# Splitting keys, values, queries and the output projections' weights once, in the first phase, and keeping both parts in DRAM

## The chip, the cores and the metric

The kernel runs on one core of one Trainium2 chip. The metric is the device time of one execution in microseconds (us), the median of several runs. A core has TensorE (PE, matmuls; PEld is its weight load), VectorE (DVE), ScalarE (ACT), GpSimd (POOL) and SyncE (SP), which here only issues DMAs. Loads are issued on SP's queue, stores mostly on ScalarE's.

## What is computed

One block of two layers over 2048 latent tokens of 1024 channels, with 256 context tokens:

```python
# layer 0 (w_in = attn_in_w, w_out = attn_out_w)
px = modulate(x, g0, shift, scale) @ w_in       # latent; ctx the same, keys and values alone
qA, kA = rms_norm(q), rms_norm(k) per head      # 4 query heads, 2 key heads of 128; rotary positions
oA = softmax(qA kA^T / sqrt(128)) vA            # over latent and context keys
oB = rms_norm((softmax(q1 k1^T / 8) - lam * softmax(q2 k2^T / 8)) vB)   # 4 differential heads
x = x + gate0 * ((concat(oA, oB) * silu(g)) @ w_out)
# layer 1 (w_fout = fourier_out_w)
u, g = split(modulate(x, g1, shift, scale) @ fourier_in_w)
f = real(fft2(u over positions and the 256 channels of each of 4 groups))
x = x + gate1 * ((f * silu(g)) @ w_fout)
out = rms_norm(x, final_g)
```

## The kernel before

Every float32 product is made of three matmuls: both operands are split into a high part (the value rounded to the matmul's format, written by a copy) and a low part (what is left, a subtraction), and `mm3` adds high x high, low x high and high x low (lines 58 to 60). `split` (line 47) makes the parts; its arguments say which engine copies and which subtracts.

The work runs in phases, one after the other on TensorE, with the tile framework's scheduler placing instructions on each engine and each queue in program order by its own estimate, outside the attention phase:

- Phase 1, the input projections, to about 813 us. Two halves of the tokens; within a half the column chunks kva (keys and values of A), kb, vb, qa, qb, and two of the gate. An output tile of 128 tokens x 512 columns takes 24 matmuls into one of five PSUM tiles `mm`. `evac` then normalises, applies the rotary tables and transposes through TensorE (`tr`, `put_T`), and stores to DRAM: keys and queries of A and queries of B in float32 (tile `qT`), keys of B already as high and low stacked (`kTh`, `kTl`), values in float32 (tile `vv`, a ring of three shared with the streamed modulation weights `aw` and the gate tile `sg`). Most of phase 1's extra work on modulation lies here too (`ada_fill`).
- Phase 2, attention, about 814 to 1998 us: 32 steps (4 heads x 8 pairs of 128 queries), whose order on PE, ACT and DVE is written out by hand. SP's queue and GpSimd are not in that order. Keys, values and queries are loaded in float32 and split here, mostly on GpSimd (`load_split`, `load_q`, lines 488 and 508).
- Phase 3, output projection and second modulation, to about 2200 us; phase 4, the Fourier input projection, to 2511 us; phase 5, the transform over positions (`m`, `ae`, `bo` on PE; `g`, `FM` on DVE; `FL` on POOL), to 2558 us; phase 6, the last projection and norm.
- Both output projections load their weights in float32 (`load_wres`, line 736): `w0h`/`w0l` are split for phase 3, and `w1h`/`w1l` for phase 6, there after a multiplication of `wr` by layer 1's gate on GpSimd (line 747). Layer 0's gate is applied after the matmul (`gx`, line 766). Weights come in two halves of columns, c = 0 and c = 1; `out_proj` goes through all four token tiles of c = 0 first.

In phase 6, TensorE takes the projection's row blocks in the order 0, 4, 1, ...; block 4 needs the row `uy`, which needs the four small loads `gy` and then a DMA of that row into `u` (lines 1087 to 1104).

Of the kernel before, what the change touches and what calls it, by code (L numbers as in the profile page):

```python
# [89 lines left out]
def block_kernel(ctx: ExitStack, tc: tile.TileContext, a):  # L90
# [12 lines left out]
    kA_d = dt_("kA", [P, 2, L])  # L103
    kB_d = dt_("kB", [P, 4, 2, L])
    qA_d = dt_("qA", [P, 4, N])
    qB_d = dt_("qB", [P, 4, N])
    vA_d = dt_("vA", [P, 2, LT, P])
    vB_d = dt_("vB", [P, 4, LT, P])
# [138 lines left out]
    with ExitStack() as ph:  # L247
# [9 lines left out]
        vvp = ph.enter_context(tc.tile_pool(name="p1v", bufs=3, reuse_waits="tile"))  # L257
# [71 lines left out]
        def put_T(src, dsts, t, stack=False):  # L329
# [14 lines left out]
            o = wk.tile([P, 4, P], F32, name="qT", tag="qT", bufs=2)  # L344
            S.copy(o[:, 0:nh, :], tr[:, 0:nh, :])
            st(dsts[:, :, t * P:(t + 1) * P], o[:, 0:nh, :])

        def evac(kind, ps, t, rp):

            if kind in ("kva", "qa"):  # L350
# [7 lines left out]
                if kind == "kva":  # L358
                    v = vvp.tile([P, 512], F32, name="vv", tag="vv")
                    S.copy(v[:, 0:256], ps[:, 256:512])  # L360
                    st(vA_d[:, :, t, :], v[:, 0:256].rearrange("p (h d) -> p h d", h=2))
# [8 lines left out]
            else:  # L370
                v = vvp.tile([P, 512], F32, name="vv", tag="vv")
                S.copy(v, ps)
                st(vB_d[:, :, t, :], v.rearrange("p (h d) -> p h d", h=4))
# [15 lines left out]
        def ada_fill(n):  # L389
# [6 lines left out]
            del later[:n]  # L396

        chunks = [("kva", COL_KVA), ("kb", COL_KB), ("vb", COL_VB), ("qa", COL_QA), ("qb", COL_QB),
                  ("g", COL_G), ("g", COL_G + 512)]
        for half in range(2):  # L400
# [5 lines left out]
            for kind, col in chunks:  # L406
                whi, wlo = load_w(col)
                for src, g in groups:
# [17 lines left out]
                    for i in range(4 if src == 0 else 2):  # L426
# [7 lines left out]
                        if kind == "vb" and src == 0:  # L434
                            ada_fill(1)

# [38 lines left out]
    with ExitStack() as ph:  # L475
# [12 lines left out]
        def load_split(pool, src, name, eng=(None, None)):  # L488

            hs, ls = [], []  # L490
            for i in range(3):
                lo = pool.tile([P, KP], F32R, name=name + "l", tag="kv")
                ld(lo.bitcast(F32), src[:, i * KP:(i + 1) * KP])
                hi = pool.tile([P, KP], F32R, name=name + "h", tag="kv")
                split(nc, hi, lo, lo.bitcast(F32), eng[0] or Q, eng[1] or Q)
                hs.append(hi)
                ls.append(lo)
            return hs, ls
# [9 lines left out]
        def load_q(rows, tag, eng=(None, None)):  # L508

            ql = qp.tile([P, QT], F32R, name="ql", tag=tag + "l")  # L510
            n = P // len(rows)
            for r, src in enumerate(rows):
                ld(ql[r * n:(r + 1) * n, :].bitcast(F32), src)
            qh = qp.tile([P, QT], F32R, name="qh", tag=tag + "h")
            split(nc, qh, ql, ql.bitcast(F32), eng[0] or Q, eng[1] or Q)
            return qh, ql
# [140 lines left out]
        def load_keys(h, eng=(None, None)):  # L657
            if h % 2 == 0:
                hd["kA"] = load_split(kp, kA_d[:, h // 2, :], "kA", eng)
            hd["kB"] = [load_stack(kB_d[:, h, c, :], "kB") for c in range(2)]  # L660

        def load_values(h):
            if h % 2 == 0:
                hd["vA"] = load_split(vp, vA_d[:, h // 2].rearrange("p t d -> p (t d)"), "vA")
            hd["vB"] = load_split(vp, vB_d[:, h].rearrange("p t d -> p (t d)"), "vB")

        def load_qs(h, pr, eng=(None, None)):
            qsl = slice(pr * QT, (pr + 1) * QT)
            return (load_q([qA_d[:, h, qsl]], "qa", eng),
                    [load_q([qB_d[c * 64:(c + 1) * 64, h, qsl]] * 2, f"qb{c}", eng) for c in range(2)])  # L670
# [7 lines left out]
        tasks, pairs, items, qs = [], [], [], [load_qs(0, 0, (S, V))]  # L678

        def begin(n):  # L680

            h, pr = steps[n]
            if pr == 0:
                load_keys(h, (S, V) if n == 0 else (None, None))
# [51 lines left out]
    def load_wres(pool, gpool, pools, src, l, order, lo_eng):  # L736
# [4 lines left out]
        for c in range(2):  # L741
            cs = slice(c * 512, (c + 1) * 512)
# [495 lines left out]
```

## Time and profile before

| | |
|---|---|
| Median of 3 runs | 2757.02 us (2750.46, 2757.02, 2762.67) |
| Profiled execution, its own time | 2757.23 us |
| Its span, first to last instruction | 2755.5 us |
| Mean granted TensorE clock | 0.971 of full |
| Busy: TensorE, VectorE, ScalarE, GpSimd | 94%, 66%, 51%, 46% |
| HBM read, written | 220.59 MB, 83.95 MB |

The span is what the rows below are read from; the profiled execution's own time is 1.7 us more. Busy time of an engine is a mean over phases with different limits, so the rows are taken by phase.

### The profile page before, as it was taken

What the parts mean: (1) busy time and instruction counts of PE and PEld (TensorE: products, weight loads), DVE (VectorE), ACT (ScalarE), POOL (GpSimd) and SP (SyncE); (2) the same over time, 40 slices, a digit from 0 to 9 for tenths busy, and PEclk for the clock granted to TensorE, in tenths of its full rate; (3) what the DMA queues carried; (4) which work ended last, traced back from release to release, by engine and by line L of the source; (5) the groups of instructions that cost most, each with busy time, mean ns of one, the idle gap of its engine ahead of it and who ended that gap; (6) DMA issues with size and microseconds to landing.
All of it is one profiled execution on the core that took longest, in us unless ns stands there. A gap on an engine that the chain in (4) does not pass through costs nothing. (4 is left out here: it accounts for less than half of the span.)

```text
span 2755.5 us, 44386 instructions
## 1 busy us (share of the span) xinstructions
PE 2595.3 (94%) x15209; PEld 2257.9 (82%) x15209; DVE 1808.4 (66%) x3855; ACT 1416.1 (51%) x3742; POOL 1259.4 (46%) x1216
## 2 busy tenths in 40 slices
PE   4889999999998999999999999999899899988898
PEld 2778887787877999999989999999778788777687
DVE  6653634747318888888888888888864535464654
ACT  3531222512227888788878888888733522121212
POOL 3121331224218666766887777766432322245200
PEclk7899999999999999999999999999999999999899
DMA  9346345364420001100120001000386767663442
GB/s 302 113 136 171 111 127 190 107 167 134 153 89 20 20 19 55 35 19 20 51 72 20 20 21 60 19 20 15 115 280 216 234 203 225 215 196 118 142 142 92
DMA packets 233457, 307.49 MB, mean 112 GB/s; under 512 B 21552, under 2 KB 134912, under 8 KB 233232
## 3 DMA queue, kind: packets, MB, share of 16 engines
q1 hardware_dynamic: 131536, 224.89, 25.8%
q10 hardware_dynamic: 97472, 75.55, 8.8%
q0 software_dynamic: 4224, 4.21, 0.7%
q8 instruction: 121, 1.98, 0.3%
q14 instruction: 104, 0.85, 0.1%
HBM read 220.59 MB, written 83.95 MB: 111 GB/s over the span
## 5 line engine op out<-in xcount | busy, mean ns | idle before, releaser
L543 DVE TENSOR_REDUCE m<-s 128x1 f32<-128x512 f32 (+1 forms) x960 | 578.5, 632 | 167.4 <-PE s L535 162.9
L555 ACT ACTIVATE e<-s,nm 128x512 f32<-128x512 f32 (+1 forms) x960 | 615.1, 654 | 53.0 <-DVE nm L547 49.7
L639 ACT CAST th<-ptr 128x512 fp32r<-128x512 f32 x576 | 340.8, 592 | 138.1 <-PE ptr L635 123.2
L643 DVE TENSOR_TENSOR tl<-ptr,th 128x512 fp32r<-128x512 f32 x576 | 379.2, 681 | 37.3 <-ACT th L639 37.3
L635 PE MATMUL ptr<-ident,e 128*128 128x128 f32 x2304 | 349.0, 274 | 20.4 <-DVE tl L643 14.2
L597 POOL TENSOR_TENSOR e<-e 128x768 f32<-128x768 f32 x189 | 342.8, 1843 | 0.0
L635 PEld LDWEIGHTS ptr<-ident,e 128*128 128x128 f32 x2304 | 271.5, 141 | 49.2 <-issue 8.4
L535 PE MATMUL s<-kB,qh 128*128 128x512 f32 (+1 forms) x768 | 284.5, 380 | 7.3 <-ACT e L555 7.3
L51 POOL TENSOR_SCALAR whi<-wraw 128x1024 fp32r<-128x1024 f32 (+1 forms) x104 | 122.5, 1181 | 360.8 <-PE mm L59 156.3
L58 PE MATMUL mm<-whi,ghi 128*128 128x512 f32 x688 | 270.8, 397 | 7.7 <-ACT vv L360 5.5
L60 PE MATMUL mm<-whi,glo 128*128 128x512 f32 x688 | 272.2, 397 | 3.8 <-DVE glo L54 3.8
L59 PE MATMUL mm<-wlo,ghi 128*128 128x512 f32 x688 | 270.8, 395 | 0.0
L594 POOL TENSOR_SCALAR e<-e,rs 128x768 f32<-128x768 f32 x192 | 171.0, 913 | 216.8 <-DVE rs L570 216.8
L535 PE MATMUL s<-kB,ql 128*128 128x512 f32 (+1 forms) x768 | 251.4, 340 | 0.0
L312 POOL TENSOR_TENSOR t<-qn,rope 128x256 f32<-128x256 f32 (+1 forms) x128 | 116.7, 934 | 263.1 <-issue 107.7
L54 DVE TENSOR_TENSOR wlo<-wraw,whi 128x1024 fp32r<-128x1024 f32 (+1 forms) x104 | 137.0, 1321 | 150.3 <-POOL whi L51 150.2
L555 ACT ACTIVATION_READ_ACCUMULATOR e<-s,nm 128x1 f32 x960 | 201.9, 210 | 0.0
L594 POOL TENSOR_SCALAR e<-e,c 128x768 f32<-128x768 f32 x189 | 169.1, 912 | 25.9 <-DVE c L578 17.4
L58 PE MATMUL pv<-th,vAh 128*128 128x256 f32 x576 | 170.7, 296 | 0.2 <-ACT oT L608 0.2
L58 PE MATMUL pv<-th,vBh 128*128 128x256 f32 x576 | 165.4, 287 | 0.0
L59 PE MATMUL pv<-tl,vAh 128*128 128x256 f32 x576 | 161.7, 281 | 0.0
L60 PE MATMUL pv<-th,vAl 128*128 128x256 f32 x576 | 161.6, 281 | 0.0
(353 smaller groups left out, 6489.9 us busy)
## 6 DMA issues: line engine op xcount, KB each, us to landing
wraw<-in_w_in SPq DMA_DIRECT2D x56, 512.0 KB
hraw<-h SPq DMA_DIRECT2D x96, 256.0 KB
aw<-in_adaT SPq DMA_DIRECT2D x64, 256.0 KB
g<-sg ACTq DMA_DIRECT2D x64, 256.0 KB
gl<-g SPq DMA_DIRECT2D x64, 256.0 KB
wraw<-in_wg SPq DMA_DIRECT2D x64, 256.0 KB
kB<-kB SPq DMA_DIRECT2D x24, 384.0 KB
awr<-in_adaT SPq DMA_DIRECT2D x32, 256.0 KB
```

The lines of the kernel that those rows point to most:

```text
L54: (lo_eng or nc.vector).tensor_tensor(out=lo, in0=src, in1=hi.bitcast(F32), op=ALU.subtract)
L58: nc.tensor.matmul(out, lh, rh, start=start, stop=False)
L59: nc.tensor.matmul(out, lh, rl, start=False, stop=False)
L60: nc.tensor.matmul(out, ll, rh, start=False, stop=stop)
L535: T.matmul(ps[:, c - o:c - o + cw], l, r[c // KP][:, k:k + cw], start=(j == 0), stop=(j == len(self.terms) - 1))
L543: V.tensor_reduce(out=self.m3[:, i:i + 1], in_=self.segs[i][:, 0:SEG[i][1]], axis=AX.X, op=ALU.max)
L555: S.activation(self.e[:, o:o + w], self.segs[i][:, 0:w], AF.Exp, bias=self.nm, accum_out=self.s3[:, i:i + 1])
L594: eng.tensor_scalar(out=self.e[:, sg], in0=self.e[:, sg], scalar1=by, scalar2=1.0, op0=ALU.mult, op1=ALU.mult)
L597: eng.tensor_tensor(out=onto[:, sg], in0=onto[:, sg], in1=self.e[:, sg], op=ALU.add)
L635: T.transpose(self.tr[:, k, i, :], self.p.es[i][:, kt * P:(kt + 1) * P], ident)
L639: S.copy(self.th, self.tr.rearrange("p k i q -> p k (i q)"))
L643: V.tensor_tensor(out=self.tl, in0=self.tr.rearrange("p k i q -> p k (i q)"), in1=self.th.bitcast(F32), op=ALU.subtract)
```

## The change

Keys and queries of A, queries of B, and all values are split in phase 1, straight from PSUM, and both parts are stored. `w_out` and `w_fout` are loaded, split and stored too: one tile of 128x512 for each of 32 output tiles of phase 1's second half (`wout_fill`, in the chunks kva, kb, qa and qb). Attention and the output projections load both parts and split nothing. Layer 1's gate is now applied after the matmul, as layer 0's is. The ring that holds `vv` grows from three buffers to four and serves six kinds of tile: `vvh`, `vvl`, `wol`, `woh`, `aw`, `sg`.

```diff
-    kA_d = dt_("kA", [P, 2, L])
+    kA_d = pair_("kA", [P, 2, L])          # two DRAM tiles: name + "h", name + "l"
...
-        vvp = ph.enter_context(tc.tile_pool(name="p1v", bufs=3, reuse_waits="tile"))
+        vvp = ph.enter_context(tc.tile_pool(name="p1v", bufs=4, reuse_waits="tile"))
...
-            o = wk.tile([P, 4, P], F32, name="qT", tag="qT", bufs=2)
-            S.copy(o[:, 0:nh, :], tr[:, 0:nh, :])
-            st(dsts[:, :, t * P:(t + 1) * P], o[:, 0:nh, :])
+            hl = [wk.tile([P, 4, P], F32R, name=nm, tag="qT", bufs=2)[:, 0:nh, :] for nm in ("qTh", "qTl")]
+            split(nc, *hl, tr[:, 0:nh, :], S)
+            for o, dst in zip(hl, dsts):
+                st(dst[:, :, t * P:(t + 1) * P], o.bitcast(F32))
+
+        def put_v(src, dsts, t, nh):
+            hl = [vvp.tile([P, 512], F32R, name=nm, tag="vv")[:, 0:nh * P] for nm in ("vvh", "vvl")]
+            split(nc, *hl, src, S)
+            for o, dst in zip(hl, dsts):
+                st(dst[:, :, t, :], o.bitcast(F32).rearrange("p (h d) -> p h d", h=nh))
...
+        def wout_fill(n):
+            for l, i, src in wouts[:n]:
+                lo = vvp.tile([P, 512], F32R, name="wol", tag="vv")
+                ld(lo.bitcast(F32), src)
+                hi = vvp.tile([P, 512], F32R, name="woh", tag="vv")
+                split(nc, hi, lo, lo.bitcast(F32), S)
+                for dst, o in zip(wo_d[l], (hi, lo)):
+                    st(dst[i], o.bitcast(F32))
+            del wouts[:n]
...
                         if kind == "vb" and src == 0:
                             ada_fill(1)
+                        elif half == 1:
+                            wout_fill(1)
...
-        def load_split(pool, src, name, eng=(None, None)):
+        def load_parts(pool, srcs, name):
...
             for i in range(3):
-                lo = pool.tile([P, KP], F32R, name=name + "l", tag="kv")
-                ld(lo.bitcast(F32), src[:, i * KP:(i + 1) * KP])
-                hi = pool.tile([P, KP], F32R, name=name + "h", tag="kv")
-                split(nc, hi, lo, lo.bitcast(F32), eng[0] or Q, eng[1] or Q)
+                for ts, src, p in zip(out, srcs, "hl"):
+                    t = pool.tile([P, KP], F32R, name=name + p, tag="kv")
+                    ld(t.bitcast(F32), src[:, i * KP:(i + 1) * KP])
...
-                raw = pool.tile([P, 512], F32, name="wr", tag="wr", bufs=4)
-                ld(raw, src[kt * P:(kt + 1) * P, cs])
-                if l:
-                    Q.tensor_tensor(out=raw, in0=raw, in1=gate[:, cs], op=ALU.mult)
-                h = pools[c].tile([P, 512], F32R, name=f"w{l}h{kt}{c}", tag=f"h{kt}{c}", bufs=1)
-                lo = pools[c].tile([P, 512], F32R, name=f"w{l}l{kt}{c}", tag=f"l{kt}{c}", bufs=1)
-                split(nc, h, lo, raw, S, lo_eng[c])
+                for src, p in zip(wo_d[l], "hl"):
+                    t = pools[c].tile([P, 512], F32R, name=f"w{l}{p}{kt}{c}", tag=f"{p}{kt}{c}", bufs=1)
+                    ld(t.bitcast(F32), src[c * KT + kt])
...
-                if gate is not None:
-                    t = lp.tile([P, 512], F32, name="gx", tag="gx", bufs=2)
-                    V.tensor_tensor(out=t, in0=ps, in1=gate[:, cs], op=ALU.mult)
-                    ps = t
-                add.tensor_tensor(out=x[i][:, cs], in0=ps, in1=x[i][:, cs], op=ALU.add)
+                t = lp.tile([P, 512], F32, name="gx", tag="gx", bufs=2)
+                V.tensor_tensor(out=t, in0=ps, in1=gate[:, cs], op=ALU.mult)
+                add.tensor_tensor(out=x[i][:, cs], in0=t, in1=x[i][:, cs], op=ALU.add)
```

The scheduler gives the queues and GpSimd another order. At the end of phase 1, SP's queue held this before (`wraw` is a weight chunk of phase 1; `kAl`, `kB`, `vAl`, `vBl`, `ql` are attention's loads):

```order
L493 DMA kAl<-kA 128x768 x3
L504 DMA kB<-kB 128x768 x7
L285 DMA wraw<-in_w_in 128x2x512
L493 DMA vAl<-vA 128x768 x3
L493 DMA vBl<-vB 128x768
L513 DMA ql<-qA 128x256
L493 DMA vBl<-vB 128x768 x3
```

and after the change this, the first row being the last weight chunk of phase 1 (a load of 128x768 float32 is 384 KB):

```order
L290 DMA wraw_7174<-in_w_in 128x2x512
L518 DMA vAh_7546<-vAh_70 128x768
L518 DMA vAl_7548<-vAl_71 128x768
L518 DMA vAh_7550<-vAh_70 128x768
L518 DMA vAl_7552<-vAl_71 128x768
L518 DMA vAh_7554<-vAh_70 128x768
L518 DMA vAl_7556<-vAl_71 128x768
L518 DMA vBh_7558<-vBh_72 128x768
L518 DMA vBl_7560<-vBl_73 128x768
L518 DMA kAh_7446<-kAh_63 128x768
L518 DMA kAl_7448<-kAl_64 128x768
L518 DMA kAh_7450<-kAh_63 128x768
```

Before, the keys stood ahead of a last `wraw` and of the values; now eight loads of values stand ahead of the keys, and the last of phase 1's weights ahead of both.

Where phase 6 begins, SP's queue held this before:

```order
L745 DMA wr<-in_w_fout 128x512
L1081 DMA fing<-in_final_g 128x1024
L745 DMA wr<-in_w_fout 128x512
L1089 DMA gy<-g_89 1x512
L745 DMA wr<-in_w_fout 128x512 x2
L1089 DMA gy<-g_90 1x512
L1089 DMA gy<-g_91 1x512
L1089 DMA gy<-g_92 1x512
L1096 DMA gl<-g_88 128x512
L1104 DMA u<-uy 1x16x32 x2
```

and after the change this, the first row being the last of 16 loads in a row of w1h and w1l for c = 1 (256 KB each):

```order
L769 DMA w1l_30141<-wo1l 128x512
L1098 DMA fing<-in_final_g 128x1024
L1106 DMA gy<-g_98 1x512
L1106 DMA gy<-g_99 1x512
L1106 DMA gy<-g_100 1x512
L1106 DMA gy<-g_101 1x512
L1113 DMA gl<-g_97 128x512
L1129 DMA xr<-x_103 128x1024
L1129 DMA xr<-x_104 128x1024
L1129 DMA xr<-x_105 128x1024
L1129 DMA xr<-x_106 128x1024
L1121 DMA u<-uy 1x16x32 x2
```

Four loads of float32 weights that stood between the small loads are gone; sixteen loads of parts stand ahead of `fing` and of all `gy`, and four loads of `xr` (512 KB each) ahead of the first rows of `u`.

GpSimd's own order in the first half of phase 5, where `FL` are its outputs of the transform, was this:

```order
L747 TENSOR_TENSOR wr<-wr,gate_29674 128x512 x2
L54 TENSOR_TENSOR w1l_29680<-wr,w1h_29679 128x512
L747 TENSOR_TENSOR wr<-wr,gate_29674 128x512
L1056 COPY FM_29238<-g_29296 128x1
L747 TENSOR_TENSOR wr<-wr,gate_29674 128x512
L1054 TENSOR_TENSOR FL<-g_29298,g_29299 128x256 x2
L1057 COPY FL_29239<-g_29298 128x1
L54 TENSOR_TENSOR w1l_29687<-wr,w1h_29686 128x512
L1056 COPY FM_29238<-g_29341 128x1
L54 TENSOR_TENSOR w1l_29694<-wr,w1h_29693 128x512
L747 TENSOR_TENSOR wr<-wr,gate_29674 128x512
L54 TENSOR_TENSOR w1l_29701<-wr,w1h_29700 128x512
```

and is this:

```order
L1073 COPY FM_29641<-g_29699 128x1
L1071 TENSOR_TENSOR FL<-g_29701,g_29702 128x256 x2
L1074 COPY FL_29642<-g_29701 128x1
L1073 COPY FM_29641<-g_29744 128x1
L1071 TENSOR_TENSOR FL<-g_29746,g_29747 128x256 x2
L1074 COPY FL_29642<-g_29746 128x1
L1073 COPY FM_29641<-g_29789 128x1
L1071 TENSOR_TENSOR FL<-g_29791,g_29792 128x256 x2
L1074 COPY FL_29642<-g_29791 128x1
```

The multiplications of `wr` and the subtractions for `w1l`, which stood between the parts of the transform, are gone.

## Rows read from the trace of the kernel before

**Rows 1.** First part of the page: busy time, share of the span, instructions.

```profile
PE 2595.3 (94%) x15209; PEld 2257.9 (82%) x15209; DVE 1808.4 (66%) x3855; ACT 1416.1 (51%) x3742; POOL 1259.4 (46%) x1216
```

**Rows 2.** Windows by stage: length, busy PE PEld DVE ACT POOL, clock, DMA, GB/s.

```profile
430.00:813.00 383.00, 369.65 (x1692) 302.53 (x1691) 179.22 (x411) 99.27 (x289) 94.89 (x98) 0.99 0.45 138
...
860.00:1950.00 1090.00, 1081.47 (x8134) 1015.97 (x8133) 940.56 (x2034) 908.10 (x2459) 783.10 (x746) 1.00 0.10 30
1950.00:2010.00 60.00, 44.53 (x291) 39.16 (x290) 46.93 (x92) 35.57 (x76) 29.13 (x22) 0.90 0.60 198
...
2511.00:2571.00 60.00, 39.33 (x234) 34.15 (x232) 42.06 (x76) 12.92 (x26) 45.57 (x48) 0.84 0.46 158
2571.00:2756.00 185.00, 175.65 (x753) 142.83 (x753) 96.81 (x226) 40.36 (x81) 0.64 (x1) 0.97 0.35 116
```

**Rows 3.** Timeline of SP's queue before attention: start, length, instruction, count.

```profile
735.15 1.53 SPq L493 DMA_DIRECT2D kAl<-kA  x3
...
813.53 1.27 SPq L493 DMA_DIRECT2D vAl<-vA  x3
```

**Rows 4.** Timeline of TensorE from the last projection matmul into attention.

```profile
813.34 0.39 PE L60 MATMUL mm<-ghi,wlo 128*128 128x512 f32 x1
813.57 0.39 PE L535 MATMUL s<-kAh,qh 128*128 128x512 f32 x1
...
816.85 0.28 PE L535 MATMUL s<-kAh,ql 128*128 128x256 f32 x1
818.90 0.50 PE L535 MATMUL s<-kAh,qh 128*128 128x512 f32 x1 [1.77 <-ACT e L555]
```

**Rows 5.** DMA view, 810 to 830 us: GB/s in 40 slices of 0.5 us.

```profile
GB/s 361 8 0 0 0 0 0 0 12 160 203 277 209 350 389 410 410 418 422 381 31 33 0 0 0 0 63 297 215 301 363 424 387 399 166 6 0 0 0 0
```

**Rows 6.** Timeline of GpSimd: the first split of values.

```profile
817.16 0.83 POOL L51 TENSOR_SCALAR vAh<-vAl 128x768 fp32r<-128x768 f32 x1 [44.22 <-PE s L535]
```

**Rows 7.** Windows at the end of attention: columns as in the windows by stage.

```profile
1950.00:1955.00 5.00, 5.00 (x40) 4.66 (x39) 4.63 (x12) 4.35 (x12) 3.12 (x4) 1.00 0.16 56
...
1960.00:1965.00 5.00, 2.89 (x22) 2.22 (x20) 3.08 (x3) 5.00 (x15) 5.00 (x4) 1.00 0.92 245
...
2005.00:2010.00 5.00, 1.80 (x7) 1.23 (x6) 3.34 (x7) 1.11 (x2) 2.30 (x2) 0.86 1.03 409
```

**Rows 8.** GpSimd's part of the weight split there: busy, mean ns, idle before.

```profile
L54 POOL TENSOR_TENSOR w0l<-wr,w0h 128x512 fp32r<-128x512 f32 x16 | 23.5, 1496 | 25.2 <-ACT w0h L49 25.2
```

**Rows 9.** Groups of GpSimd, 2508 to 2575 us (Fourier stage).

```profile
L747 POOL TENSOR_TENSOR wr<-wr,gate 128x512 f32<-128x512 f32 x16 | 21.7, 1372 | 28.4 <-DMA wr<-in_w_fout 28.4
L1054 POOL TENSOR_TENSOR FL<-g,g 128x256 f32<-128x256 f32 x16 | 12.4, 798 | 4.9 <-DVE g L1051 4.9
L54 POOL TENSOR_TENSOR w1l<-wr,w1h 128x512 fp32r<-128x512 f32 x8 | 11.2, 1404 | 0.3 <-ACT w1h L49 0.3
```

**Rows 10.** Waits of TensorE, 2508 to 2580 us: total, times, longest.

```profile
PE m L58 <- DVE g L1051: 6.6, 3, 3.2
PE mm L58 <- ACT uh L49: 5.9, 2, 4.3
```

**Rows 11.** Timeline of VectorE: two pairs of FM.

```profile
2540.42 2.03 DVE L1053 TENSOR_TENSOR FM<-g,g 128x256 f32<-128x256 f32 x2
...
2551.91 0.92 DVE L1053 TENSOR_TENSOR FM<-g,g 128x256 f32<-128x256 f32 x2
```

**Rows 12.** Timeline of TensorE: last transform matmul, second block of the last projection.

```profile
2557.97 0.37 PE L60 MATMUL m<-sh,O1L 128*128 128x256 f32 x1
...
2571.22 0.80 PE L58 MATMUL mm<-w1h,uh 128*128 128x512 f32 x1 [4.29 <-ACT uh L49]
```

**Rows 13.** ScalarE's cast of an existing split, 0 to 813 us, by line.

```profile
L49 ACT CAST kTh<-tr 128x512 fp32r<-128x512 f32 x18 | 10.6, 588 | 44.6 <-DMA kB<-kTh 21.1 <-PE tr L333 15.6 <-PE mm L60 7.8
```

**Rows 14.** A store's issue on ScalarE's queue: min/median/max ns, first and last start.

```profile
L373 ACTq DMA_DIRECT2D vB<-vv x18: 520/521/584, 245.9 to 628.1; - x18
```

**Rows 15.** VectorE's gate product of layer 0, 2010 to 2200 us, by line.

```profile
L766 DVE TENSOR_TENSOR gx<-mm,gate 128x512 f32<-128x512 f32 x32 | 21.9, 688 | 34.9 <-PE mm L60 34.9
```

More of the change, by code (lines that the diff above doesn't have):

```diff
@@ L101, in dt_, with pair_ @@
         return dram.tile(shape, F32, name=name, tag=name)
-    kA_d = dt_("kA", [P, 2, L])
+    def pair_(name, shape):
+        return dt_(name + "h", shape), dt_(name + "l", shape)
+    kA_d = pair_("kA", [P, 2, L])
     kB_d = dt_("kB", [P, 4, 2, L])
[L105 to L108, printed above, removed]
+    qA_d = pair_("qA", [P, 4, N])
+    qB_d = pair_("qB", [P, 4, N])
+    vA_d = pair_("vA", [P, 2, LT, P])
+    vB_d = pair_("vB", [P, 4, LT, P])
+    wo_d = [pair_(f"wo{l}", [2 * KT, P, 512]) for l in range(2)]
     g1_d = [dt_(f"g1{i}", [P, N]) for i in range(8)]
@@ L396, in ada_fill @@
             del later[:n]
+        wouts = [(l, c * KT + kt, a[nm][kt * P:(kt + 1) * P, c * 512:(c + 1) * 512])
+                 for l, nm in enumerate(("w_out", "w_fout")) for c in range(2) for kt in range(KT)]
+        def wout_fill(n):
[7 more added lines that the diff above has]
+            del wouts[:n]
         chunks = [("kva", COL_KVA), ("kb", COL_KB), ("vb", COL_VB), ("qa", COL_QA), ("qb", COL_QB),
@@ L506, in load_stack, with load_q @@
             return out
[L508 to L516, printed above, removed]
+        def load_q(parts, tag, times=1):
+            out = []
+            n = P // times
+            for src, p in zip(parts, "hl"):
+                t = qp.tile([P, QT], F32R, name="q" + p, tag=tag + p)
+                for r in range(times):
+                    ld(t[r * n:(r + 1) * n, :].bitcast(F32), src)
+                out.append(t)
+            return out
         class Task:
@@ L677, in block_kernel @@
         rest = early.steps(tp)
-        tasks, pairs, items, qs = [], [], [], [load_qs(0, 0, (S, V))]
+        tasks, pairs, items, qs = [], [], [], [load_qs(0, 0)]
         def begin(n):
@@ L733, in block_kernel, with load_wres @@
                         qs.append(load_qs(*steps[n + 1]))
-    def load_wres(pool, gpool, pools, src, l, order, lo_eng):
+    def load_wres(gpool, pools, l, order):
         gate = gpool.tile([P, D], F32, name=f"gate{l}", tag="gate", bufs=1)
@@ L781, in block_kernel @@
         fp = ph.enter_context(tc.tile_pool(name="p3f", bufs=2, reuse_waits="tile", side="right"))
-        wres = load_wres(wp, lp, (wp, w1p), a["w_out"], 0, range(KT), (Q, Q))
+        wres = load_wres(lp, (wp, w1p), 0, range(KT))
         def second_mod(x, t):
```

39 lines of the change are left out of this document (17 added, 22 removed).

## The prediction

> **What bounds the kernel now.** I read the page's busy times first: TensorE is busy 94% of the span [rows 1], GpSimd far less, so work taken from GpSimd counts only where TensorE waits for it. The windows by stage say where that is [rows 2]. In phase 1's second half TensorE idles 13 of 383 us, in steady attention 8.5 of 1090 us. The idle time lies at the seams: 15.5 of 60 us where attention ends, 20.7 of 60 us from the Fourier transform into the last projection. A gain must come from these seams, and the reader should look at the same places for losses, since the loads behind them are what the change alters.
>
> **Seam of phase 1 and attention (a cost).** Now there is none: the last projection matmul starts at 813.34 and the first score matmul 0.23 us later [rows 4], because the keys were loaded at 735 us, and only the values wait for the projection to end, at 813.53 [rows 3]. After the change the values' loads wait for the same matmul (their SBUF is phase 1's), and the keys stand behind eight of them in SP's in-order queue. TensorE needs the first kAh and kAl, the ninth and tenth loads of 0.393 MB (128 x 768 x 4 bytes).
>
> The trace times this pattern. Four loads issued from 813.53 moved from about 814.5 to 820.0, and the plateau was some 410 GB/s [rows 5]; the first could be used at 817.16 [rows 6]. Six more at 0.393/0.41 = 0.96 us each are 5.8 us: the first keys land at about 825.8, 12.2 us late. The third pair, four loads later, lands at 829.6. The first task's scores, which ended at 817.1 [rows 4], need it for their last two segments (three matmuls of 512 columns at 0.23 us and three of 256 at half of that, 1.0 us; the one at 816.85 is the last), so they end at about 830.9: **+14 us**. What is late next is the first softmax and all that follows; the later first steps wait on ScalarE's exponentials (1.77 us before the second task [rows 4]), a chain that moves along and hides none of it. Bounds: +10 if the freed GpSimd, which now splits values at the head of its queue [rows 6], gives some of the start-up back; +17 if TensorE, after 12 us of idling, runs its next 3.5 us of scores at the lower clock, as it does at 2571.22, where the first matmul of this size takes 0.80 us instead of 0.39 [rows 4, 12].
>
> By the Trainium skill's page "DMA: Bandwidth & Descriptors", section "Where 436 GB/s comes from", a core's loads from HBM are bound near 358 GB/s. By that the six loads would take 6.6 us instead of 5.8 and the ten 1.4 us longer than I count, and the term would be about +15. The slices at 410 to 422 GB/s, with nothing on the other cores, say the measurement [rows 5], and the sum goes by it.
>
> **Steady attention.** Per step three splits leave GpSimd, and SP's queue gets five more loads. TensorE idles 8.5 us in 1090 [rows 2], so the gain is between 0 and -8.5; most of these waits need not be GpSimd's: **-2**. The DMA share is 0.10 there, so doubled query loads are hidden.
>
> **End of attention (a gain).** In 1960 to 1965 ScalarE and GpSimd are both busy for all 5 us while TensorE gets 2.9 [rows 7]; they split w0h and w0l, 1.5 us per subtraction on GpSimd [rows 8], among the factors that the last steps wait for. That work goes. In its place 32 loads of 256 KB, 8.4 MB instead of 4.2, come in two rows. The first 16 can run from about 1950, where DMA has a share of 0.16, and take 4.2/0.41 = 10 us. The other 16 meet the loads of 2005 to 2010, already at 1.03 and 409 GB/s [rows 7], but c = 1 is needed only four tiles (22 us) after c = 0. Of 15.5 us idle, a third was casts and subtractions: **-4**; bounds -8 (half of the idle time) and +4 (the first 16 delay the loads of `ol` and `gl`, half of their 10 us).
>
> **Fourier transform into the last projection (a gain).** GpSimd is the busiest engine here, 45.6 of 60 us [rows 2]. The gate product takes 1.37 us each and the subtraction for w1l 1.40 [rows 9]: 12 and 8 of them before the last transform matmul are 28 us of an in-order queue into which the 16 FL (0.80 us each) are laced. `g` cannot be written again before FL has read it, and TensorE waits 6.6 us for `g` [rows 10]. VectorE is slowed besides: a pair of FM takes 2.03 us while GpSimd works and 0.92 late, when GpSimd has little left [rows 11]. TensorE's clock, 0.84 over the 60 us [rows 2], falls with its idling. Without this queue VectorE, 42 us busy now [rows 2], saves some 5 us on eight pairs of FM; I place the last transform matmul at 2544 instead of 2557.97 [rows 12], 14 us earlier (between 2541 and 2549, that is 9 to 17).
>
> Part of that is lost again. The second row block started at 2571.22, 13.2 us behind that matmul [rows 12]. It needs `u`'s row of `uy`. After the change `gy` stands behind 12 loads of c = 1 that need the tables' SBUF, 3.1 MB (7.7 us at 0.41), and `fing` (0.5 MB, 1.3 us); and the row's DMA behind four `xr` (2.1 MB, 5.1 us). With about 2.6 us to the first landing, as at 813.53 [rows 5, 6], and 1.3 us of split, that is 18 us instead of 13.2. So the block starts near 2562: -9, of which I take **-8**. Bounds: -15 (transform at 2541, small loads not delayed) and +3 (2549, and the row 25 us behind it).
>
> **Last projection.** 32 gate products of 0.69 us [rows 15] are added on VectorE, which is busy 97 of 185 us [rows 2]; TensorE covers them. Only the last tile's shows: **+1**. Without that cover they would cost 22 us.
>
> **Phase 1 (a cost).** VectorE gets 118 subtractions from new splits: 82 of 512 columns at 0.69 (a gate product, also from PSUM [rows 15]) and 36 of 256 at about half: 70 us, 45 of them in the second half, where it is busy 179 of 383 [rows 2]. ScalarE gets 32 casts of 0.59 [rows 13] and 150 store issues of 0.52 [rows 14], 97 us in all; there it is busy 99 of 383 and its queue has as much room. The sums fit; order is the risk. Eight kva tiles of the second half each use all four buffers of the ring, and a fill lives for a load (3 us; 3.6 for 384 KB [rows 3, 6]), a cast and a subtraction (1.3), an issue (0.5) and a store's landing (3): 8 us, against 5.4 for the tile's 24 matmuls at 0.227 [rows 4]. The lag, 2.6 x 8 = 21 us, is covered by four more PSUM tiles (22 us), just. ScalarE already waits 21.1 us for kTh's stores [rows 13], and now every q tile has that ring. **+3**; bounds 0 and +12 (half of the lag not covered).
>
> **The sum** against the profiled execution's own time: 2757.2 + 14 - 2 - 4 - 8 + 1 + 3 = **2761 us**. That execution agrees with the median, 2757.02. This kernel's runs spread by some 0.4%, and a measurement can tell about 0.5% (14 us) from no change; so this is within it.
>
> **The rivals.**
> - *The fill's ring stalls phase 1* (slower). From the point where the lag of the kva tiles passes the 22 us of PSUM cover, each further us of a fill's life costs 8. At a life of 9.5 us it would be 33 - 22 = +11 over my term, and waits of SP's queue for a ring buffer hold `wraw` behind them: 2772 to 2785, say 2775. For it: the waits for stores now [rows 13]. Against: GpSimd's and SP's room there. Chance 0.2.
> - *The loads of the parts are the new bound at both later seams* (slower). +4 and +3 at their bounds instead of -4 and -8: 2761 + 8 + 11 = 2780. For it: DMA at 409 GB/s at 2005 to 2010 [rows 7]. Against: c = 0 is loaded early in both. Chance 0.1.
> - *The seams pay in full* (faster). The transform's end moves 17 us and the block follows as it does now, attention's end gives 8 and its waits 6, the keys cost 10: 2757.2 + 10 - 6 - 8 - 15 + 1 + 0 = 2739. For it: GpSimd's 45.6 of 60 us [rows 2]. Against: the order of SP's queue. Chance 0.13.
>
> **How the numbers follow.** The forecast has 0.57; its own range is 2746 to 2774, from its terms' bounds taken as independent. With the rivals the range is 2742 to 2784. Faster by over 0.5% (below 2743): the third rival, 0.13. Slower by over 0.5% (above 2771): both first rivals and a part of the forecast, 0.31. Within: 0.56.
>
> **What would show it.** In the profile after: TensorE idle for some 12 us from the last projection matmul, waiting for loads of kA; the first task's scores ending 17 us behind it; GpSimd with a few FL alone in the transform and the second row block starting 18 us after the last transform matmul; attention's steps as long as before; waits of `mm` in phase 1 of a few us at most. Wrong would be: keys in place at once, TensorE waiting for PSUM in the second half's kva tiles, or the last projection starting no earlier than 190 us before the end.

## The result

The changed kernel takes 2779.18 us, the median of 6 runs, against 2756.37 us of 6 runs before on the same chip: a ratio of 1.0077, 95% interval 1.0059 to 1.0096. It is 0.8% slower. One of the six runs took 4358.33 us, at a mean granted clock of 0.555 where the other five had 0.968 to 0.971; the ratio leaves it out. The profiled execution took 2779.38 us with a span of 2777.4, against 2757.23 and 2755.5 before.

The first part of the page after, beside [rows 1]:

```profile
PE 2595.3 (93%) x15209; PEld 2250.0 (81%) x15209; DVE 1845.9 (66%) x3991; ACT 1410.2 (51%) x3736; POOL 1042.9 (38%) x948
```

GpSimd lost 216 us of work, and TensorE still had the same matmuls to do and a longer span to do them in. To see where, I set the two traces side by side by matmul: the lag is by how much the same matmul starts later than before. This table holds it for all kernels of this study, in us (ends and starts from the timelines of TensorE; "pv" is the first product with values, "head 4" the one at 1733.3; the second row block of e8 to e12 has one output tile of the first block less ahead of it).

```
matmul            before    after   e1    e2    e3    e4    e5    e6    e7    e8    e9   e10   e11   e12
last projection    813.3    29.6  28.6   8.2  15.2   0.0  31.3  32.6  67.3  30.2   9.6   3.1   8.7  16.0
first scores       813.6    42.4  28.6  21.2  23.3   7.8  31.3  33.5  67.3  30.2  31.6  17.5   8.7  16.0
first pv           850.7    45.7  29.6  24.3  28.9  12.8  33.7  81.4  68.0  31.3  35.7  36.6   9.7  17.7
pv, head 4        1733.3    33.1  16.9  11.7  29.6  12.1  21.2  68.8  66.2  18.6  22.7  37.2  -2.5  19.1
out projection    1998.3    27.3  10.2  12.7  22.6  12.1  16.4  61.9  69.0  12.3  23.6  38.6  -0.4  21.7
transform starts  2511.4    27.5   6.9  12.7  18.7   7.3  11.1  58.0  67.6   4.0  20.2  33.8  -7.6  17.0
transform ends    2558.0     9.5 -10.9  12.4   0.6   7.2  -6.9  39.9  67.6 -13.9   2.6  15.6 -25.6  -1.1
2nd row block     2571.2    22.0   1.3  15.0  12.3   8.7   2.0  48.6  69.3 -11.6   4.9  17.7 -23.3   1.0
last matmul       2746.5    21.6   1.4  15.4  11.8   8.4   2.1  49.3  69.8 -10.8   5.3  18.8 -22.4   2.3
```

**Phase 1 lost 29.6 us.** Windows of the kernel after (length, busy PE PEld DVE ACT POOL, clock, DMA share, GB/s), which also answer to [rows 2]:

```profile
500.00:600.00 100.00, 94.03 (x430) 74.11 (x429) 67.14 (x173) 43.78 (x130) 28.50 (x34) 0.98 0.66 200
600.00:700.00 100.00, 88.40 (x389) 70.75 (x388) 58.64 (x138) 23.77 (x82) 20.41 (x19) 0.97 0.89 282
...
890.00:1980.00 1090.00, 1088.24 (x8205) 1022.19 (x8205) 937.36 (x2052) 915.25 (x2482) 657.64 (x549) 1.00 0.15 46
1980.00:2040.00 60.00, 51.04 (x342) 44.41 (x342) 48.24 (x114) 34.16 (x75) 13.37 (x12) 0.97 0.69 236
2539.00:2595.00 56.00, 35.48 (x236) 30.67 (x235) 31.60 (x72) 5.66 (x13) 16.57 (x24) 0.83 0.69 238
```

Before, the first two windows read:

```profile
500.00:600.00 100.00, 98.42 (x468) 80.27 (x467) 62.91 (x149) 34.35 (x106) 34.34 (x38) 1.00 0.46 125
600.00:700.00 100.00, 96.56 (x444) 78.80 (x443) 61.38 (x146) 22.99 (x95) 34.66 (x36) 1.00 0.51 148
```

No compute engine but TensorE is near full in 600 to 700: VectorE is busy 58.6, ScalarE 23.8. The DMA engines are at a share of 0.89, but such a share alone did not stop TensorE: e11, the last but one kernel below, has a stretch of phase 1 at 0.84 whose lag grows by 0.7 us only:

```profile
400.00:500.00 100.00, 93.24 (x409) 75.67 (x408) 50.81 (x99) 20.54 (x44) 60.86 (x80) 0.97 0.84 287
```

TensorE is idle for 11.6 us here, and the waits say that the order of the queues has a large part in it. Waits of ScalarE and SP in the kernel after, 500 to 740 us (total, times, longest):

```profile
ACT woh L49 <- DMA wol<-in_w_fout: 21.5, 6, 12.2
...
ACT woh L49 <- DMA wo0l<-wol: 6.8, 2, 3.8
...
SPq L413 <- DMA wo0h<-woh: 23.9, 9, 5.5
...
SPq L413 <- DMA wo1h<-woh: 18.6, 7, 4.7
```

ScalarE waits in order for a fill's load, with evictions behind it; SP waits 42.5 us at the fills' loads (L413) until earlier fills are stored and a ring buffer is free. So SP comes late to the loads of `aw`, which need the same ring. Its queue in the kernel after, and below it the same place before:

```profile
612.61 0.33 SPq L413 DMA_DIRECT2D wol<-in_w_out  x1
621.57 26.95 SPq L183 DMA_DIRECT2D aw<-in_adaT  x14
```

```profile
594.38 29.20 SPq L178 DMA_DIRECT2D aw<-in_adaT  x14
```

The loads of `aw` take 27 to 29 us to issue in both, but SP comes to them 27.2 us later now. TensorE's largest wait of phase 1 is for `wlo`, the low part of a weight chunk. The chunk was there, for GpSimd had made its high part `whi` 12 us before; it was the subtraction on VectorE that came late. After, and then before:

```profile
636.42 1.05 POOL L51 TENSOR_SCALAR whi<-wraw 128x1024 fp32r<-128x1024 f32 x1 [27.67 <-PE mm L60]
...
648.68 1.22 DVE L54 TENSOR_TENSOR wlo<-wraw,whi 128x1024 fp32r<-128x1024 f32 x1
...
649.95 0.79 PE L59 MATMUL mm<-wlo,ghi 128*128 128x512 f32 x1 [6.82 <-DVE wlo L54]
```

```profile
623.48 1.05 POOL L51 TENSOR_SCALAR whi<-wraw 128x1024 fp32r<-128x1024 f32 x1 [31.86 <-PE mm L60]
...
625.01 2.05 DVE L54 TENSOR_TENSOR wlo<-wraw,whi 128x1024 fp32r<-128x1024 f32 x1
```

From `whi` to `wlo` it is 12.3 us after and 1.5 before. In front of `wlo`, VectorE's queue holds subtractions `vvl` of new values and sums over `aw`. From 618.9 to 648.7 us they wait for stores of earlier `vvl` and for loads of `aw`, both of which live in the shared ring:

```profile
DVE vvl L54 <- DMA vBl<-vvl: 12.6, 5, 6.0
DVE aw L187 <- DMA aw<-in_adaT: 4.7, 5, 2.3
```

Behind the wait TensorE runs at a granted clock of 0.50 (650 to 654 us), so that the lag grows by more than the 6.8 us of the wait.

**The seam came as forecast.** SP's queue, and TensorE's answer to [rows 4]:

```profile
843.12 0.34 SPq L518 DMA_DIRECT2D vAh<-vAh  x1
...
846.76 0.40 SPq L518 DMA_DIRECT2D vBl<-vBl  x1
847.94 0.32 SPq L518 DMA_DIRECT2D kAh<-kAh  x1
```
```profile
842.93 0.39 PE L60 MATMUL mm<-ghi,wlo 128*128 128x512 f32 x1
855.93 0.76 PE L558 MATMUL s<-kAh,qh 128*128 128x512 f32 x1 [12.62 <-DMA kAh<-kAh]
```

**Attention gave 12.5 us back**, against 2 forecast. In the windows by 100 us, before has three with idle time; in the changed kernel every window from 900 to 1900 has TensorE busy 100.00. Before first:

```profile
1100.00:1200.00 100.00, 97.81 (x730) 91.92 (x729) 83.48 (x183) 81.22 (x220) 74.32 (x71) 0.98 0.10 30
1400.00:1500.00 100.00, 94.85 (x702) 88.59 (x702) 85.99 (x174) 79.14 (x215) 77.89 (x74) 0.98 0.13 38
1700.00:1800.00 100.00, 98.81 (x745) 92.64 (x744) 88.24 (x187) 82.72 (x225) 77.58 (x74) 1.00 0.09 28
```
```profile
1400.00:1500.00 100.00, 100.00 (x759) 93.83 (x757) 85.59 (x186) 84.10 (x229) 59.87 (x51) 1.00 0.37 119
```

These three are the changes of heads, where GpSimd splits a new head's values between its own parts of the softmax. Their idle time is 2.2 + 5.2 + 1.2 = 8.5 us, the whole of steady attention's 8.5 [rows 2]. TensorE waits there for GpSimd's `e` (2.2 us) and for VectorE's `tl` (5.1 and 1.2); the clock of 0.98 in two of them is worth some 4 us more (2% of 200 us, an estimate).

**The transform gained 18 us, and the block behind it lost 12.5.** TensorE and SP in the kernel after:

```profile
2567.50 0.27 PE L60 MATMUL m<-sh,O1L 128*128 128x256 f32 x1
...
2593.22 0.80 PE L58 MATMUL mm<-w1h,uh 128*128 128x512 f32 x1 [14.04 <-ACT uh L49]
```
```profile
2579.94 2.25 SPq L1106 DMA_DIRECT2D gy<-g  x4
...
2583.35 2.83 SPq L1129 DMA_DIRECT2D xr<-x  x4
2586.27 1.23 SPq L1121 DMA_DIRECT2D u<-uy  x2
```

The last transform matmul starts 9.5 us late instead of 27.5, but the second row block starts 25.7 us behind it where it was 13.2 [rows 12]. Where the gain comes from is read from TensorE first, over the transform before and after:

```profile
2511.40:2558.30 46.90, 34.02 (x217) 30.74 (x215) 30.86 (x60) 9.05 (x20) 38.04 (x42) 0.85 0.38 126
```
```profile
2538.90:2567.80 28.90, 27.18 (x217) 24.85 (x215) 21.15 (x51) 4.00 (x10) 12.60 (x20) 1.00 0.62 206
```

Of the 18 us, 11.2 are idle time that is gone (12.9 before, 1.7 after), and 6.8 are the same 217 matmuls at a granted clock of 1.00 instead of 0.85. Of the idle time 6.6 us were waits for `g` [rows 10], which the kernel after does not have. VectorE's pairs of FM have a part in it: by line, 2520 to 2570 us after and 2510 to 2560 us before, an FM took 610 ns instead of 933, some 4.5 us on 14 of them:

```profile
L1070 DVE TENSOR_TENSOR FM<-g,g 128x256 f32<-128x256 f32 x12 | 6.9, 610 | 0.0
```
```profile
L1053 DVE TENSOR_TENSOR FM<-g,g 128x256 f32<-128x256 f32 x14 | 12.5, 933 | 0.2
```

### The profile page after: what moved, and what is told of

Its sections match the earlier page's. It is cut to its first block, busy times and chain, and to the rows that moved or that the text cites. A ratio compares the mean times of both kernels' runs of the same rounds, so it can differ in the third digit from the quotient of the medians.

```text
span 2777.4 us, 44879 instructions
## 1 busy us (share of the span) xinstructions
PE 2595.3 (93%) x15209; PEld 2250.0 (81%) x15209; DVE 1845.9 (66%) x3991; ACT 1410.2 (51%) x3736; POOL 1042.9 (38%) x948
## 3 DMA queue, kind: packets, MB, share of 16 engines
q10 hardware_dynamic: 142880, 110.17, 12.5%
## 5 line engine op out<-in xcount | busy, mean ns | idle before, releaser
L58 PEld LDWEIGHTS mm<-whi,ghi 128*128 128x128 f32 x688 | 131.6, 191 | 40.0 <-DVE vvl L54 6.1
```

Source lines behind the costliest of these rows:

```text
L58: nc.tensor.matmul(out, lh, rh, start=start, stop=False)
```

## The experiments

Times are medians; a ratio is to runs of the kernel before on the same chip. Kernels with a single run show no time difference below some 0.5%; their lags, taken inside one execution, are what I read. Where there are more runs, the profiled one need not lie at the median: that of e12 is 6.7 us above it, those of e9 and e11 are 5.6 and 5.2 below, so a lag that one of them alone shows can be off by as much.

**e1 and e4: what makes the keys wait.** As the buffers are laid out in the built programs, a ring of four reaches to byte 178912 of a partition, and attention's 13 key buffers begin at 177120, so a key's load has to wait for the last gate tile; twelve begin at 180192, and a ring of three ends at 176864. e1 is the changed kernel with

```
-P2K = 13
+P2K = 12
```

> The changed kernel with attention's key pool cut from 13 buffers to 12, nothing else. Theory (memory overlap): the ring's fourth buffer lies over the first buffer of the key pool, so the keys wait for the last gate tile of phase 1; with 12 buffers the pool no longer reaches the ring, the keys are loaded during phase 1 again, the 12.6 us wait of TensorE for kAh goes and the seam costs under 2 us instead of 16: about 2763 us, with phase 1 as late as in the changed kernel (last projection matmul near 843). Rival (bandwidth): the doubled loads are what is late, and TensorE still waits some 12 us there: about 2779. The buffer taken away could cost up to 3 us at each of three changes of head.

e4 is the kernel before with the larger ring alone:

```
-        vvp = ph.enter_context(tc.tile_pool(name="p1v", bufs=3, ...
+        vvp = ph.enter_context(tc.tile_pool(name="p1v", bufs=4, ...
```

> The kernel before with the ring of phase 1 grown from three to four buffers, nothing else. Theory (memory overlap): that alone puts the key loads behind the first value loads, TensorE waits for keys after the last projection matmul, the first task's scores end some 8 to 10 us later than before, and the whole takes about 2766. Phase 1 itself is as before or up to 1 us shorter. Rival (the doubled loads are needed for the stall): no wait at the seam and 2757.

e1: 2757.59 us, ratio 1.0003 [0.9988, 1.0019]; TensorE goes on without a gap:

```profile
841.95 0.39 PE L60 MATMUL mm<-ghi,wlo 128*128 128x512 f32 x1
842.18 0.39 PE L558 MATMUL s<-kAh,qh 128*128 128x512 f32 x1
```

e4: 2765.61 us, with no lag in phase 1 and 7.8 us at the first scores. One buffer makes the seam and one takes it away: its cause is the place of the buffers, and the SP order that follows from it. The parts' bytes set its size: 7.8 us with whole loads (e4), 13.0 with parts (e2). e1 alone undoes the change's whole loss.

**e2 and e3: who costs phase 1 its time.** e2 is the changed kernel with the weights loaded and split late as before; e3 the kernel before with the weights' fills alone (and the ring of four).

```
e2:  -                        elif half == 1:
     -                            wout_fill(1)
e3:  +                        elif half == 1:
     +                            wout_fill(1)
```

> The changed kernel with the output projections' weights left as before (no fills in phase 1, weights split in phases 3 and 6, layer 1's gate on the weights); keys, queries and values split in phase 1, ring of four. Theory (fills load the DMA engines in phase 1's second half): its lag against the kernel before falls from 29.6 us at the last projection matmul to 8 to 13, the late weights before the qa chunk are gone, and phases 5 and 6 are as before (transform 47 us, second row block 13 us behind it): about 2757 + 10 + 16 - 12 - 2 = 2769. Rival (the doubled stores of keys, values and queries and the fuller ring are enough): the lag stays at 20 us or more, and the time is 2780 or more.

> The kernel before with only the weights' part of the change (fills in phase 1's second half, parts loaded in phases 3 and 6, gate after the matmul) and the ring of four; keys, queries and values as before. Theory (fills load the DMA engines): phase 1 ends 8 to 15 us late, less than the sum in the changed kernel, since the stores are not doubled; attention as before with its three waits at changes of head; transform 17 us shorter and the second row block 24 us behind it, 6 us gained in all. The keys stand behind values here too (ring of four), some 9 us at the seam: about 2757 + 12 + 9 - 4 - 6 = 2768. Rival (stores of keys, values and queries are the whole lag): phase 1 ends under 4 us late, 2756 or so.

e2 2772.68, e3 2769.78 us. Phase 1: 8.2 us without fills, 15.2 us with fills alone, 29.6 us with both: the two share the ring and cost 6 us more together. The wait for `wlo` above is in neither of the two. The attention rows settle another point: from the first pv to head 4, e2 gains 12.6 us, e3 loses 0.7. The gain in attention is that of the split of keys, queries and values. The transform's gain is that of the fills: e3 -18.1, e2 -0.3.

**e5: the row transfers on another queue.** From e1:

```
-                ld(gy[b:b + 1, :], g2_d[4 + b][0:1, cs])
+                Q.dma_start(out=gy[b:b + 1, :], in_=g2_d[4 + b][0:1, cs])
-                    ld(u[0:1, :], uy[b - 4:b - 3, :])
+                    Q.dma_start(out=u[0:1, :], in_=uy[b - 4:b - 3, :])
```

> The changed kernel with a key pool of 12 buffers (as e1_keys12) and, in the last projection, the small loads gy and the row DMAs of u issued on GpSimd's queue instead of SP's, so that they no longer stand behind the loads of w1h and w1l. Theory (SP's order is what the second row block waits for): it starts 9 to 13 us behind the last transform matmul instead of 25, and the time falls from 2757.6 to about 2744. Rival (the DMA engines are full there, whatever the queue): it still starts 20 us or more behind, and the time stays within 5 us of 2757.6.

2754.91 us, ratio 0.9987 [0.9974, 1.0]. My theory fell: the block still started 22.1 us behind the transform. But the edit changed the issue less than I meant it to. On GpSimd's queue the four `gy` stood behind its last `FL`, and were issued from 2559.16, 8.1 us behind the transform (11.9 in e1, on SP):

```profile
2557.50 1.71 POOL L1071 TENSOR_TENSOR FL<-g,g 128x256 f32<-128x256 f32 x2 [1.29 <-DVE g L1068]
2559.16 2.04 POOL L1106 DMA_DIRECT2D gy<-g  x4
2567.41 0.99 POOL L1121 DMA_DIRECT2D u<-uy  x2 [6.22 <-issue]
```

So SP's order is not tested alone. What e5 does show is that without a bulk load ahead of them in their queue the rows are still slow: 6.7 us from the first issue of `gy` to the last landing, 5.8 from the issue of `u` to the matmul. The windows of e5 (columns as above) show the engines full:

```profile
2560.00:2565.00 5.00, 1.77 (x7) 1.09 (x5) 0.00 (x0) 0.00 (x0) 1.20 (x3) 0.84 1.06 389
2565.00:2570.00 5.00, 0.00 (x0) 0.00 (x0) 0.68 (x1) 0.00 (x0) 2.47 (x6) 0.50 1.04 393
```

The Trainium skill's page "DMA: Bandwidth & Descriptors", section "Issuing engines are not separate DMA queues", says that transfers of all issuing engines share the same 16 DMA engines. This run agrees: 6.7 us from issue to landing for four rows of 2 KB on a queue without bulk loads.

**e8: hold the loads instead.** From e1: the second half of layer 1's weights, the `xr` tiles and `fing` are queued behind a group's last row.

```
-                    ld(u[0:1, :], uy[b - 4:b - 3, :])
+                    row = ld(u[0:1, :], uy[b - 4:b - 3, :])
...
+            with tc.issue_after(row.ins):
+                if g == 0:
+                    load_half(wres[0], (wp, w1p), 1, KORDER, 1)
                 for i in range(4):
                     x = xp.tile([P, D], F32, name="xr", tag="xr")
```

> The changed kernel with twelve key buffers, in which the last phase's second half of the weights (4.2 MB), its first four x tiles and the final gain are queued on SP behind group 0's last u row. If those loads fill the transfer engines (share 1.02 to 1.06 over 2555 to 2570 in the two runs before) and so hold the one-row transfers back, then the last block's first matmul comes 10 to 15 us behind the transform's last instead of 22 to 25 us, and the time is 2743 to 2748 us against 2757.6 us of the same kernel without the hold. Rival: the rows are slow by themselves (four transfers in a chain, each some 5 to 9 us however empty the engines are): the start stays 20 us or more behind, and the second half of the weights then comes later too, 2757 us or above.

2749.13 us, ratio 0.9961 [0.9946, 0.9975]. The share of the DMA engines while the rows move, SP's rows and TensorE's start in e8:

```profile
2555.00:2560.00 5.00, 0.37 (x1) 0.37 (x2) 1.07 (x2) 1.04 (x2) 0.00 (x0) 0.70 0.04 12
```
```profile
2557.13 1.22 SPq L1123 DMA_DIRECT2D u<-uy  x2
```
```profile
2544.06 0.27 PE L60 MATMUL m<-sh,O1L 128*128 128x256 f32 x1
...
2559.63 0.80 PE L58 MATMUL mm<-w1h,uh 128*128 128x512 f32 x1 [5.49 <-ACT uh L49]
```

From the rows' issue to the matmul that needs them it is 2.5 us here; in e1, with 306 to 388 GB/s moving, it was 7.2 (2565.27 to 2572.49). The start is 15.6 us behind the transform instead of 25.4, and the second half of the weights is still in time. By steps, from the transform to the issue of `gy`, to the issue of `u`, to the block: 11.9, 6.3 and 7.2 us in e1; 9.2, 3.9 and 2.5 in e8. So 7.2 of the 9.8 us come from the transfers themselves and 2.7 from the earlier issue. Together with e5 this shows that the bulk loads, which the change made free to start earlier, hold the small transfers back, mostly in the DMA engines and to a smaller part in SP's queue.

**e6 and e7: fills elsewhere, and copies alone.** e6 is e5 with the fills moved to the 16 gate tiles of the second half, two at each; e7 the kernel before with three DRAM-to-DRAM copies of 256 KB at each fill's place.

```
e6:  +                            if half == 1:
     +                                wout_fill(2)
e7:  +                for d in junk_d[3 * l:3 * l + 3]:
     +                    Q.dma_start(out=d[i], in_=src)
```

> As e5_row_queue, and the 32 fills of the output projections' weights moved from the kva, kb, qa and qb tiles of phase 1's second half to its 16 gate tiles, two fills each, where VectorE, ScalarE and the DMA engines have the least to do. Theory (the fills collide with the stores and rings of the key and query tiles): phase 1 ends 8 to 11 us late, as without fills, instead of 29, and the time is about 2744 - 18 = 2726. Rival (the fills cost what they cost anywhere, or the keys now come late behind them): phase 1 or the seam behind it stays 20 us or more late, and the time is about 2744.

> The kernel before with extra traffic alone: at each kva, kb, qa and qb tile of phase 1's second half three copies of 256 KB from DRAM to DRAM are issued on GpSimd's queue, as many transfers of that size as a fill has (one load, two stores), with no ring, no split and nothing on SP's or ScalarE's queues; the copies' results are not used. Theory (DMA engines): stores and loads of phase 1 land later, and the last projection matmul comes 8 us or more late (15.2 in e3_fillonly): 2764 or more. Rival (ring and queue order): under 3 us late, 2757 to 2760.

e6: 2804.97 us, ratio 1.0163 [1.0144, 1.0183]. The lag stays near 9 us up to the last query tile and then grows to 32.6 in the gate tiles, with the DMA engines at a share of 0.66 to 0.80. ScalarE's waits in e6, 760 to 846 us:

```profile
ACT woh L49 <- DMA wol<-in_w_out: 28.6, 9, 5.0
ACT woh L49 <- DMA wol<-in_w_fout: 13.6, 4, 3.7
```

TensorE waits 11.4 us for ScalarE's `sg` there. And the values' loads come behind fills on SP, so the first pv is 81.4 us late. In both places where fills went through ScalarE and SP, those two stood still for them. e7: 2827.26 us, no test: the copies depend on nothing and were issued from the first us on, and phase 1's start paid for them.

**e9 and e10: only the second projection's fills, on GpSimd.** e9 is e8 with `w_out` split late as before and the 16 fills of `w_fout` on GpSimd and its queue, one at each gate tile of the second half, in buffers that key and query tiles leave free; e10 the same on the kernel before (keys, queries and values whole).

```
+                lo = wk.tile([P, 512], F32R, name="wol", tag="qn", bufs=2)
+                Q.dma_start(out=lo.bitcast(F32), in_=src)
+                hi = wk.tile([P, 512], F32R, name="woh", tag="qT", bufs=2)
+                split(nc, hi, lo, lo.bitcast(F32), Q, Q)
+                for dst, o in zip(wo_d[1], (hi, lo)):
+                    Q.dma_start(out=dst[i], in_=o.bitcast(F32))
```

> As the run with the held loads, but only the second output projection's 16 weight tiles are split early, on GpSimd and GpSimd's own queue, one at each of half 2's gate tiles and in buffers that the key and query tiles leave free; the first projection's weights are loaded and split at the end of attention as in the kernel before. If it is the fills (loads, splits on ScalarE and stores of 32 tiles) that cost phase 1 some 20 of its 29 us, and the transform's gain hangs on the second projection alone: last projection matmul 8 to 12 us late, attention and its end 12 us gained, transform 17 us gained, the block's start as in the run with the held loads: 2730 to 2742 us. Rival: fills cost phase 1 the same wherever they stand, since the transfer engines carry them (25 us late at the last projection matmul): 2748 us or above.

> The kernel before with these 16 early splits alone and the held loads: keys, queries and values are kept whole in DRAM and split in attention as before. If the split of keys, queries and values costs phase 1 some 8 us and gives attention 12 us back at the changes of heads, this lies 2 to 6 us above the run before it: 2735 to 2746 us, with no gain inside attention, the transform's gain of 17 us and a phase 1 within 4 us of the kernel before. Rival: the attention's gain came from something else than the moved splits (the buffers, the shift of phase 1): it then shows here too, and the time is below 2735 us.

e9: 2769.71 us, ratio 1.0036 [1.0024, 1.0048]; e10: 2779.59, 1.0079 [1.0061, 1.0097]. Both times miss, and phase 1 is as expected in both: 9.6 and 3.1 us, so these 16 fills off ScalarE and SP cost 1.4 us (9.6 against e2's 8.2) and 3.1 us. What I had not seen is the seam. GpSimd makes a fill each 6.2 us (load, split, stores; the mean of the 16), more than a tile's 5.4, and its last one comes after the projection's end (e9):

```profile
843.38 0.62 POOL L51 TENSOR_SCALAR woh<-wol 128x512 fp32r<-128x512 f32 x1 [7.26 <-DMA wol<-in_w_fout]
```
```profile
845.19 0.77 PE L558 MATMUL s<-kAh,qh 128*128 128x512 f32 x1 [21.88 <-DMA kAh<-kAh]
```

Keys behind values again. Inside attention e9 gains 13.0 us up to head 4 and e10 loses 0.6: the shift of phase 1 does nothing for it.

**e11 and e12: the same fills in the first half.**

```
-                            if half == 1:
+                            if half == 0:
                                 wout_fill(1)
```

> The same kernel as the one with 16 early splits on GpSimd (keys, queries and values split, held loads), with the 16 splits moved from half 2's gate tiles to half 1's. If the 22 us at the seam came from the splits' buffers, which were free only at 835 to 843 us while the first keys need their memory, then the keys are loaded before the last projection matmul again and attention starts without a wait: last projection matmul 8 to 11 us late, attention gains 12 us between its heads, the transform 17 us: 2734 to 2746 us. Rival: the seam waits for something that comes with the split keys and values themselves (more and smaller loads): the wait of 10 us or more stays and the time is 2752 us or above.

> The same with keys, queries and values whole in DRAM and split in attention, as in the kernel before. If their early split costs phase 1 some 8 us and gives back 12 us in attention, this kernel loses 4 us against the run beside it: phase 1 within 3 us of the kernel before, no gain inside attention, transform 17 us gained, 2738 to 2750 us. Rival: the early split of keys, queries and values is worth nothing or costs time: this kernel is as fast as the one beside it or faster.

e11: **2740.77 us, ratio 0.9942 [0.9926, 0.9957]**, faster than both kernels. At the seam TensorE goes on without a wait:

```profile
822.02 0.39 PE L60 MATMUL mm<-ghi,wlo 128*128 128x512 f32 x1
822.25 0.39 PE L558 MATMUL s<-kAh,qh 128*128 128x512 f32 x1
```

The wait that e9 has there is gone, with the split keys and values still there: it came with the late fills, whose buffers lie in the built program where attention's keys go. Place and lateness of the fills moved together, so the two are not told apart. e12: 2754.01 us, ratio 0.999 [0.9979, 1.0001], 13 us above e11 and outside what I expected. Of its 16.0 us in phase 1, 12.6 arise between 404 and 501 us, beside the fills, where e11 loses 0.7: GpSimd waits 25.5 us for the fills' loads there (8.9 in e11, each from 400 to 530 us), and a wait for `whi` of 4.5 us reaches TensorE. This is one execution, 6.7 us above its kernel's median. So the two kernels differ in more than the split, and the price of the split is better read from e2, e9 and e11: 8.2 us in phase 1 (9.6 and 8.7 with 16 fills), for 12 to 13 back in attention.

## Why the prediction came out as it did

The time lies in the range of 2742 to 2784, 18 us above the forecast. It lies there by the rivals' width: the forecast's own range ended at 2774, and the case given the highest chance, within 0.5%, did not come. (By the root of the sum of squares the terms' bounds give 2749 to 2778, not 2746 to 2774; the time is outside of that too.) By its steps:

- **Phase 1, the step that failed.** The term was +3, bounds 0 to +12; it measured +29.6. The working gave the eight kva tiles of the second half a lag of 21 us, covered by 22 us of PSUM tiles. Three things were wrong in it. The cost did not sit there: these tiles, from 501 to 565 us, added the 3 us of the forecast (5.3 to 8.4). It grew later, by 4.4 in the kb tiles, by 10.5 around 645 us, where `wlo` stood on VectorE behind `vvl` and `aw`, and by 5.4 in the query tiles. I counted room on VectorE, on ScalarE and in SP's queue as if it could be used in any order; all three work in order here, and what one instruction waits for, all behind it wait for. And 8 us of it are no fill at all but the split of keys, queries and values (e2), 6.3 of the changed kernel's lag being there at 431 us, before its second half begins. The first rival had the shared ring and the "waits of SP's queue for a ring buffer" (42.5 us), and deserved more than 0.2; but it put the loss into the kva tiles and behind `wraw`, and TensorE's largest wait was for neither.
- **The seam.** +14, measured 42.4 - 29.6 = 12.8 for the first scores and 16.1 up to the first pv. The wait was forecast as 12.2 and is 12.62. The 3.3 us more are the lower clock, which the prediction had as a bound: the scores behind the wait, 855.9 to 862.6 us, ran at a granted 0.52. e4 and e1 show its cause, which the prediction had only as an order of loads.
- **Steady attention.** -2, measured -12.5, beyond the bound of -8.5. "Most of these waits need not be GpSimd's" was wrong: all are at the changes of heads, and all went. e2, e3, e9 and e10 show whose gain it is.
- **End of attention.** -4, measured -5.8 (33.1 to 27.3). e9, with `w_out` split late, shows +0.9 there.
- **Transform and the block behind it.** Together -8, measured 22.0 - 27.5 = -5.5: the transform -18 instead of -14, the block 25.7 us behind it instead of 18. The 18 us were 9.0 to the issue of `gy`, 5.1 for `xr` and 3.9 for landing and split. In the kernel after it is 12.4 to the issue of `gy` (sixteen loads stood ahead, not twelve), 6.3 from there to the issue of `u`, and 7.0 from there to the block. I took the loads ahead of the row as a queue on SP alone; e5 and e8 show that the full DMA engines hold the rows as well.
- **Last projection.** +1, measured -0.1 from the block's start (22.0) to the span's end (21.9); the added gate products are covered.

The errors of phase 1 (+27) and attention (-10) cancel in part, which is luck, and what is left of them makes most of the 18 us. Not explained: how the split of keys, queries and values costs phase 1 its 8 us; phases 3 and 4 take 3 to 8 us less than before in all these kernels but the changed one, e2 and e7; and why e12's fills cost 12.6 us where e11's cost 0.7.

## What to carry to other kernels

Work moved into a stage with idle engines is not free if it goes through the queues that the bound engine waits for: 32 fills through ScalarE and SP added 21 us to phase 1, and 16 on GpSimd, in buffers that other tiles leave free, 1 to 3 us in three kernels (e9, e10, e11) but 16 in a fourth (e12). No run changes the engine alone, with number and place kept. When loads lose the work that paced them, look at what small transfers they will now fill the DMA engines in front of, and hold the bulk behind them. A bigger ring or one more use of a buffer changes whose memory the next stage's first load waits for: read the layout, not only the counts.

## What the hardware showed unexpectedly

Small row transfers took 2.5 us from issue to use with the DMA engines at a share of 0.04 (e8). Issued at a share of 0.92 to 1.04, they took 7.0 and 7.2 us on SP's queue (the changed kernel, e1) and 5.8 on GpSimd's (e5). The DMA engines reach a share of 0.89 at 282 GB/s in phase 1 with its small stores, and 1.06 at 389 GB/s with whole weight tiles: the rate alone does not say how full they are. The Trainium skill's page "DMA: Bandwidth & Descriptors", section "Where 436 GB/s comes from", puts the limit of a core's HBM loads near 358 GB/s, half of a stack's 716 for each of two cores; e5's two windows of loads, 389 and 393, lie above it, and this program runs on one core alone.
